# Squares of the norms added by VectorE, and post-norm factors read from PSUM, in a two-layer hybrid decoder trunk

## The chip, the cores and the metric

The kernel runs on one core of one Trainium2 chip (trn2). The metric is the device time of one execution in microseconds (us); lower is better. A core has five engines with a queue of their own each: TensorE (PE in the profile; its weight loads are PEld), VectorE (DVE), ScalarE (ACT), GpSimd (POOL) and SyncE (SP, which here issues DMAs). They work in parallel and wait for each other by semaphores; each engine takes its own instructions strictly in the order in which the program was written out.

## The reference

A trunk of two layers (DEPTH 2) over 528 tokens (16 learned meta tokens ahead of 512) with 1024 channels. Layer 0 mixes by forgetting attention (16 heads of 64), layer 1 by a gated DeltaNet (8 heads of 128); each layer ends in a gated FFN of width 2816 with a causal convolution. Every mixer and every FFN stands between two RMSNorms:

```python
def rmsnorm(x, g):
    xf = x.astype(jnp.float32)
    y = xf * lax.rsqrt(jnp.mean(xf * xf, axis=-1, keepdims=True) + EPS)
    return (y * g.astype(jnp.float32)).astype(x.dtype)
...
for i in range(DEPTH):
    a = rmsnorm(h, norm_mix_pre[i])
    m = forgetting_attention(a, ...) if i % 2 == 0 else gated_deltanet(a, ...)
    h = h + rmsnorm(m, norm_mix_post[i])
    f = conv_ffn(rmsnorm(h, norm_ffn_pre[i]), ffn_w_up[i], ffn_conv[i], ffn_w_down[i])
    h = h + rmsnorm(f, norm_ffn_post[i])
return h[:, N_META:]
```

## The kernel before

Activations lie transposed: 128 channels on the partitions, tokens along the free side, 8 such tiles (k = 0 to 7) for 1024 channels. The tokens are cut in two halves, of 272 and 256 columns (260 and 256 from the last mixer projection on). Each matrix product (`dense`, L312) is done in a high and a low part of both operands (`xh`, `xl` of the activations, `wh`, `wl` of the weights): three matmuls for each k, accumulated in one PSUM tile. Weights come by SP's DMAs (`w`, L284), are rounded by ACT (`wh`, L285) and their rest is made by DVE or POOL (`wl`, L292). A list of weight tiles is worked through for half 0 at once and for half 1 some tiles later (`push`, a lag of 4 or 6), so that PE has work for one half while the other half's results are finished.

Between two stages stands `boundary`, once for each half: after the attention's output projection (called boundary 1 below), after the first FFN (boundary 2), after the DeltaNet's output projection (boundary 3), and after the second FFN (the end, with no norm behind it). For a half it does the following.

- While the last projection's eight tiles `m` come out of PSUM (L465, L468 or L811 on DVE), ACT squares each (`sq`, L352; the first one goes straight into the sum, `ssq`, L349) and the squares are added into `ssq` (L353). After the eighth, `reduce` lets PE sum over the partitions (L342, into the PSUM tile `psn`).
- `inv` adds the epsilon on DVE (`nst`, L361), takes the power -0.5 on POOL (L363), lets PE spread the factors over the partitions (transposes into `psn`, L365), and ACT copies them from PSUM to SBUF (`r`, L367).
- For k = 0 to 7, DVE multiplies `m` by the post-norm's gain and `r` (`bt`, L411), adds this to the residual stream (`h`, L412), and, where a stage follows, `prenorm_tile` squares the new `h` (ACT, L352) into the next norm's sum (L353), makes `xh` (ACT, L377) and `xl` (DVE, L378). The next stage's matmuls take `xh` and `xl` as they come; the next norm's factor `r` is multiplied in only when their result leaves PSUM (`ub`, L748). That second `inv` runs after the eighth k.

`psn` tiles come from two PSUM rings of one bank each, used in turn. The program's order on each engine is set by a scheduler that plays the whole program through with its own estimates of durations; the DeltaNet stage, in addition, orders its work by a table of delays (`Flow`). So an edit in one place can move instructions elsewhere.

Of the kernel before, what the change touches and what calls it, by code (L numbers as in the profile page):

```python
# [13 lines left out]
ALU = mybir.AluOpType  # L14
# [90 lines left out]
def trunk(ctx, tc, h0, wflat, params, out):  # L105
    nc = tc.nc
# [103 lines left out]
    def ng(name, layer, k):  # L210
        c = pc[name] + layer * 8 + k
        return prm[:, c:c + 1]
# [106 lines left out]
    def tmp(name):  # L319
        return sm.tile([P, 272], F32, name=name, tag="tmp", bufs=4)  # L320

    def tmp2(name):
        return sm.tile([P, 272], F32, name=name, tag="tm2", bufs=5)

    def chunks(half):
        n = HALF[half][1]
        return (0, 128, n - 128) if n > 256 else (0, 128)
# [6 lines left out]
    class SumSq:  # L334
# [9 lines left out]
        def add(self, src, tmp=tmp):  # L344
            n, k = self.n, self.k
            self.k += 1
            if k == 0:
                self.acc = sm.tile([P, 272], F32, name="ssq", tag=f"ssq{self.half}")
                nc.scalar.activation(self.acc[:, :n], src, AF.Square)  # L349
                return  # L350
            sq = tmp("sq")
            nc.scalar.activation(sq[:, :n], src, AF.Square)  # L352
            nc.gpsimd.tensor_tensor(self.acc[:, :n], self.acc[:, :n], sq[:, :n], op=ALU.add)  # L353
            if k == KT - 1:
                self.reduce()

        def inv(self):
            half, n, ch, ps = self.half, self.n, chunks(self.half), self.ps
            w = len(ch)
            st = sm.tile([P, 8], F32, name="nst", tag=f"nst{half}", bufs=2)  # L360
            nc.vector.tensor_scalar(st[:, 0:w], ps[:, 0:w], EPS, None, op0=ALU.add)  # L361
            yst[half] = st
            nc.gpsimd.tensor_tensor(st[:, 4:4 + w], st[:, 0:w], mhalf[:, 0:w], op=ALU.pow)  # L363
            for j, c in enumerate(ch):
                nc.tensor.transpose(ps[:, 16 + c:16 + c + 128], st[:, 4 + j:5 + j].to_broadcast([P, P]), ident[:])  # L365
            r = sm.tile([P, 272], F32, name="r", tag=f"r{half}")
            nc.scalar.copy(r[:, :n], ps[:, 16:16 + n])  # L367
            return r

    def new_x(half, name):  # L370
        return take(half, name, F32R)


    def prenorm_tile(half, k, name, layer, xh, xl, ss):
        ss.add(h[half][:, k, :], tmp2)
        g = ng(name, layer, k)
        nc.scalar.activation(xh[:, k, :], h[half][:, k, :], AF.Identity, scale=g)  # L377
        nc.vector.scalar_tensor_tensor(xl[:, k, :], h[half][:, k, :], g, xh[:, k, :].bitcast(F32), op0=ALU.mult, op1=ALU.subtract)  # L378
# [21 lines left out]
        X[half] = (xh, xl, r)  # L400

    def boundary(half, m, ssm, post, pre):
        r = ssm.inv()
        n = HALF[half][1]
        last = pre is None
        if not last:
            xh, xl = new_x(half, "xh"), new_x(half, "xl")
            ss = SumSq(half)
        for k in range(KT):
            t = tmp2("bt")  # L410
            nc.vector.scalar_tensor_tensor(t[:, :n], m[:, k, :], ng(post[0], post[1], k), r[:, :n], op0=ALU.mult, op1=ALU.mult)  # L411
            nc.vector.tensor_tensor(h[half][:, k, :], h[half][:, k, :], t[:, :n], op=ALU.add)  # L412
            if not last:
                prenorm_tile(half, k, pre[0], pre[1], xh, xl, ss)
            else:
                s = max(HALF[half][0], NM)
                e = HALF[half][0] + n
                nc.sync.dma_start(out[:, k, s - NM:e - NM], h[half][:, k, s - HALF[half][0]:n])
        if not last:
            X[half] = (xh, xl, ss.inv())  # L420
# [29 lines left out]
    def out_proj(srcs, post, pre, reload, m, dropsrc):  # L450
        more = m[0] is not None
        ssm = [None, None]
        for mt in range(8):
            def fn(u, half, mt=mt):
                n = HALF[half][1]
                if m[half] is None:
                    drop(*X[half][:2])
                    m[half] = take(half, "m")
                oh, ol = srcs(half)
                ps = dense(u, half, lambda k: oh[:, k, :], lambda k: ol[:, k, :])  # L460
                if mt == 0:
                    ssm[half] = SumSq(half)
                mm = m[half][:, mt, :]
                if more:
                    nc.vector.tensor_tensor(mm, mm, ps, op=ALU.add)  # L465
                    ssm[half].add(mm)
                else:
                    nc.vector.tensor_copy(mm, ps)  # L468
                    ssm[half].add(ps)
                if mt == 4:  # L470
                    reload(half)
                if mt == 7:
                    dropsrc(half)
                    boundary(half, m[half], ssm[half], post, pre)
                    drop(m[half])
            push(nextu(), fn)
# [293 lines left out]
    def ffn(layer, post, pre):  # L770
        with ExitStack() as cx:
# [27 lines left out]
            def down(u, half, b, mt):  # L799
                n = HALF[half][1]  # L800
                j0 = sum(FB[:b])
                if b == 0 and mt == 0:
                    m[half] = take(half, "m")
                if b == 2 and mt == 0:
                    ssm[half] = SumSq(half)
                ps = dense(u, half, lambda k: acts[j0 + k, half][0], lambda k: acts[j0 + k, half][1])
                mm = m[half][:, mt, :]
                if b == 0:
                    nc.scalar.copy(mm, ps)
                else:  # L810
                    nc.vector.tensor_tensor(mm, mm, ps, op=ALU.add)  # L811
                if b == 2:
                    ssm[half].add(mm)
                    if mt == 7:
                        drop(*X[half][:2])
                        boundary(half, m[half], ssm[half], post, pre)
                        drop(m[half])
# [662 lines left out]
```

## Time and profile before

| | |
|---|---|
| time, median of 3 runs | 1604.43 us (1603.03 to 1607.17) |
| the profiled execution's own time | 1601.35 us |
| its span on the core | 1599.4 us |
| PE busy | 1525.8 us (95%) |
| DVE busy | 1123.4 us (70%) |
| ACT busy | 815.4 us (51%) |
| POOL busy | 495.8 us (31%) |
| mean granted PE clock | 0.977 |

Times in the profile are counted from the span's start. The profiled execution is 3.1 us faster than the median of the runs. A row of the timeline reads: start, duration, engine, line, operation, output and inputs, and in brackets how long the engine sat idle before it and what ended that. A row of the groups reads: line, engine, operation, names, shapes, count, then busy time and mean ns of one, then idle time before and its releaser. A row by windows gives, for a stretch, its length and the busy time of each engine with its instructions, the granted PE clock, and the DMA share.

### The profile page before, as it was taken

The numbers are of one execution on the slowest core, as the hardware profiler recorded it, in microseconds if no ns is written. First come the engines' busy times: TensorE is split into PE (matmuls) and PEld (weight loads), VectorE is DVE, ScalarE is ACT, GpSimd is POOL, SyncE is SP. The second block draws the span as 40 slices with busy tenths as digits, with TensorE's granted clock in tenths as the row PEclk, the third lists the DMA queues.
The fourth block names the chain that finished last, engine by engine and source line by source line (L and its number), as shares of the span: only waits on it lengthen the run. The fifth ranks groups of instructions, "written<-read, shape, count | busy, mean of one in ns | idle before, by whom it ended". The sixth has DMA issues, their size and how long they took to land.

```text
span 1599.4 us, 33295 instructions
## 1 busy us (share of the span) xinstructions
PE 1525.8 (95%) x12630; PEld 1486.8 (93%) x12630; DVE 1123.4 (70%) x2629; ACT 815.4 (51%) x1925; POOL 495.8 (31%) x993
## 2 busy tenths in 40 slices
PE   8999999999999999999789899899989999999996
PEld 6999999899999999999789798898989999999996
DVE  7888888948974675674978665676569864765764
ACT  6677777735643442343564456545456543432441
POOL 6434443025300010012556475654154200100112
PEclk9999999999999999999799998999999999999998
DMA  5232222422223222222323322222141323323321
GB/s 175 89 89 79 75 78 85 134 65 82 84 83 100 93 85 88 93 93 72 107 75 90 90 61 71 68 77 61 50 150 66 91 82 106 92 82 106 93 67 53
DMA packets 63327, 139.04 MB, mean 87 GB/s; under 512 B 18584, under 2 KB 31288, under 8 KB 62784
## 3 DMA queue, kind: packets, MB, share of 16 engines
q1 hardware_dynamic: 62544, 134.55, 28.1%
q8 instruction: 99, 1.62, 0.4%
q0 software_dynamic: 480, 2.15, 0.4%
q14 instruction: 60, 0.49, 0.1%
q10 hardware_dynamic: 144, 0.22, 0.0%
HBM read 131.54 MB, written 5.36 MB: 86 GB/s over the span
## 4 chain that ended last, share of the span: by engine, by line
PE 74%; DVE 11%; POOL 5%; DMA 4%; ACT 3%; issue 3%; SPq 1%; POOLq 0%; DVEq 0%; ACTq 0%
PE ps L312 65%; POOL PR L1177 2%; POOL RB L1178 2%; DVE h L412 1%; DVE bt L411 1%; DVE wl L292 1%; PE av L698 1%; DMA w<-wflat 1%; DVE cv L764 1%; DMA gcr<-gcd 1%; PE pt L678 1%; DVE xl L378 1%; ACT wh L285 1%; PE s L1277 1%; DVE qr L577 1%
## 5 line engine op out<-in xcount | busy, mean ns | idle before, releaser
L312 PE MATMUL ps<-xh,wh 128*128 128x256 f32 (+4 forms) x2464 | 717.6, 293 | 16.8 <-DVE ub L748 9.2
L312 PE MATMUL ps<-xl,wh 128*128 128x256 f32 (+4 forms) x2464 | 710.8, 289 | 3.4 <-DVE xl L378 3.0
L312 PE MATMUL ps<-xh,wl 128*128 128x256 f32 (+4 forms) x2464 | 713.6, 290 | 0.0
L312 PEld LDWEIGHTS ps<-xh,wh 128*128 128x128 f32 (+1 forms) x2464 | 469.6, 192 | 22.8 <-DVE ub L748 6.3
L312 PEld LDWEIGHTS ps<-xl,wh 128*128 128x128 f32 (+1 forms) x2464 | 471.1, 191 | 7.4 <-DVE xl L378 4.6
L312 PEld LDWEIGHTS ps<-xh,wl 128*128 128x128 f32 (+1 forms) x2464 | 471.1, 191 | 1.0
L285 ACT CAST wh<-w 128x1024 fp32r<-128x1024 f32 (+3 forms) x226 | 225.1, 997 | 189.5 <-PE ps L312 166.7
L292 DVE TENSOR_TENSOR wl<-w,wh 128x1024 fp32r<-128x1024 f32 (+4 forms) x191 | 220.6, 1156 | 99.3 <-ACT wh L285 98.7
L764 DVE SCALAR_TENSOR_TENSOR cv<-ub,prm,cv 128x256 f32<-128x256 f32 (+2 forms) x494 | 243.8, 498 | 38.4 <-ACT cv L755 29.5
L312 PE MATMUL ps<-ah,wl 128*128 128x256 f32 (+2 forms) x704 | 199.5, 284 | 0.0
L312 PE MATMUL ps<-ah,wh 128*128 128x256 f32 (+2 forms) x704 | 199.3, 283 | 0.0
L312 PE MATMUL ps<-al,wh 128*128 128x256 f32 (+2 forms) x704 | 199.1, 283 | 0.0
L755 ACT ACTIVATE cv<-ub,prm 128x256 f32<-128x256 f32 (+2 forms) x224 | 113.8, 511 | 146.3 <-DVE ub L748 146.2
L748 DVE TENSOR_TENSOR ub<-ps,r 128x256 f32<-128x256 f32 (+2 forms) x224 | 95.4, 428 | 101.5 <-PE ps L312 100.6
L353 POOL TENSOR_TENSOR ssq<-ssq,sq 128x256 f32<-128x256 f32 (+2 forms) x98 | 90.5, 926 | 144.5 <-ACT sq L352 143.0
L312 PEld LDWEIGHTS ps<-ah,wh 128*128 128x128 f32 x704 | 132.6, 189 | 0.0
L312 PEld LDWEIGHTS ps<-al,wh 128*128 128x128 f32 x704 | 132.5, 188 | 0.0
L312 PEld LDWEIGHTS ps<-ah,wl 128*128 128x128 f32 x704 | 132.4, 188 | 0.0
L751 POOL COPY cy<-ub 128x2 f32<-128x2 f32 (+1 forms) x112 | 38.0, 341 | 279.3 <-DVE ub L748 277.7
L292 POOL TENSOR_TENSOR wl<-w,wh 128x512 fp32r<-128x512 f32 x70 | 95.0, 1377 | 72.1 <-ACT wh L285 56.8
L747 POOL COPY ub<-cy 128x2 f32<-128x2 f32 (+1 forms) x112 | 31.3, 280 | 197.1 <-DVE cv L764 160.0
L786 ACT ACTIVATE gl<-cv 128x272 f32<-128x272 f32 (+2 forms) x88 | 36.7, 418 | 42.0 <-DVE cv L764 41.7
(308 smaller groups left out, 2454.5 us busy)
## 6 DMA issues: line engine op xcount, KB each, us to landing
w<-wflat SPq DMA_DIRECT2D x176, 512.0 KB, 3.5
w<-wflat SPq DMA_DIRECT2D x32, 448.0 KB, 3.3
cB<-cdram SPq DMA_DIRECT2D x16, 264.0 KB, 3.3
w<-wflat SPq DMA_DIRECT2D x16, 256.0 KB, 2.7
h<-h SPq DMA_DIRECT2D x8, 272.0 KB, 5.3
cB<-cdram SPq DMA_DIRECT2D x16, 136.0 KB, 3.0
h<-h SPq DMA_DIRECT2D x8, 256.0 KB, 5.0
AB<-dA SPq DMA_DIRECT2D x16, 128.0 KB, 3.2
```

Of the source, the lines that this page charges most:

```text
L285: nc.scalar.copy(wh[:], w32)
L292: eng.tensor_tensor(wl[:, c], w32[:, c], wh[:, c].bitcast(F32), op=ALU.subtract)
L312: tok(nc.tensor.matmul(o, w[:, a], r[:, c0:c1], start=(i == 0), stop=(i == tot - 1)))
L353: nc.gpsimd.tensor_tensor(self.acc[:, :n], self.acc[:, :n], sq[:, :n], op=ALU.add)
L747: nc.gpsimd.tensor_copy(ub[:, 0:c0], carry.pop(ft)[:, :c0])
L748: nc.vector.tensor_tensor(ub[:, c0:c0 + n], ps, r[:, :n], op=ALU.mult)
L751: nc.gpsimd.tensor_copy(c[:, :c0], ub[:, n:n + c0])
L755: nc.scalar.activation(cv, ub[:, c0:c0 + n], AF.Identity, scale=w[c0])
L764: nc.vector.scalar_tensor_tensor(cv, ub[:, i:i + n], w[i], cv, op0=ALU.mult, op1=ALU.add)
L786: nc.scalar.activation(g, cv, AF.Gelu_apprx_tanh)
L1177: nc.gpsimd.tensor_tensor(t, R3[:, 0:a, l:l + 1].to_broadcast([P, a, w]), A3[:, l:l + 1, l + 1:32].to_broadcast([P, a, w]), op=ALU.mult)
L1178: nc.gpsimd.tensor_tensor(R3[:, 0:a, l + 1:32], R3[:, 0:a, l + 1:32], t, op=ALU.subtract)
```

## The change

All 98 additions of squares into `ssq` go from POOL to DVE. The eight post-norm calls of `inv` (two halves at four boundaries) no longer let ACT copy the factors to SBUF: `bt` reads them from the PSUM tile `psn`. The six pre-norm calls keep the copy, and the power -0.5 stays on POOL. Lines behind the edits have numbers that are higher by 2 or 3: `xl` of the pre-norm is L380, `bt` L414, `h` L415, `ub` L751 in the changed kernel.

```diff
@@ SumSq.add
             nc.scalar.activation(sq[:, :n], src, AF.Square)
-            nc.gpsimd.tensor_tensor(self.acc[:, :n], self.acc[:, :n], sq[:, :n], op=ALU.add)
+            nc.vector.tensor_tensor(self.acc[:, :n], self.acc[:, :n], sq[:, :n], op=ALU.add)
@@ SumSq.inv
-        def inv(self):
+        def inv(self, copied=True):
...
+            if not copied:
+                return ps[:, 16:16 + n]
             r = sm.tile([P, 272], F32, name="r", tag=f"r{half}")
             nc.scalar.copy(r[:, :n], ps[:, 16:16 + n])
             return r
@@ boundary
-        r = ssm.inv()
+        r = ssm.inv(False)
```

The scheduler writes the engines' orders anew. Three places are shown.

DVE at boundary 2, in the middle of half 1's eight k (a 256-column round of `bt`, `h`, `xl`), before:

```order
L411 SCALAR_TENSOR_TENSOR bt<-m_7369,prm,r 128x256
L412 TENSOR_TENSOR h_5587<-h_5587,bt 128x256
L378 SCALAR_TENSOR_TENSOR xl_10686<-h_5587,prm,xh_10685 128x256
L411 SCALAR_TENSOR_TENSOR bt<-m_7369,prm,r 128x256
L748 TENSOR_TENSOR ub<-ps,r 128x272
```

The same place after:

```order
L414 SCALAR_TENSOR_TENSOR bt<-m_7365,prm,psn 128x256
L751 TENSOR_TENSOR ub<-ps,r 128x272
L353 TENSOR_TENSOR ssq<-ssq,sq 128x256
L415 TENSOR_TENSOR h_5585<-h_5585,bt 128x256
L380 SCALAR_TENSOR_TENSOR xl_10678<-h_5585,prm,xh_10677 128x256
```

An addition stands between each `bt` and the `h` that needs it, and the first `ub` of the next stage comes one round earlier: behind the seventh `bt` of half 1 and not behind the eighth.

DVE at the start of boundary 3 (from the power's input `nst` of half 0 to half 0's first `xl`; `m` are half 1's last projection tiles, `wl` are weights of the next FFN), before:

```order
L361 TENSOR_SCALAR nst<-psn 128x3
L292 TENSOR_TENSOR wl<-w_16674,wh 128x1024
L465 TENSOR_TENSOR m_15716<-m_15716,ps 128x256 x3
L292 TENSOR_TENSOR wl<-w_16716,wh 128x1024
L411 SCALAR_TENSOR_TENSOR bt<-m_15448,prm,r 128x260 x2
L292 TENSOR_TENSOR wl<-w_16761,wh 128x1024
L412 TENSOR_TENSOR h_16192<-h_16192,bt 128x260
L361 TENSOR_SCALAR nst<-psn 128x2
L412 TENSOR_TENSOR h_16192<-h_16192,bt 128x260
L411 SCALAR_TENSOR_TENSOR bt<-m_15448,prm,r 128x260
L378 SCALAR_TENSOR_TENSOR xl_16318<-h_16192,prm,xh_16317 128x260
```

After:

```order
L292 TENSOR_TENSOR wl<-w_16662,wh 128x1024
L361 TENSOR_SCALAR nst<-psn 128x3
L353 TENSOR_TENSOR ssq<-ssq,sq 128x256
L468 TENSOR_TENSOR m_15708<-m_15708,ps 128x256
L353 TENSOR_TENSOR ssq<-ssq,sq 128x256
...
L414 SCALAR_TENSOR_TENSOR bt<-m_15440,prm,psn 128x260 x2
L415 TENSOR_TENSOR h_16184<-h_16184,bt 128x260
L292 TENSOR_TENSOR wl<-w_16704,wh 128x1024
L353 TENSOR_TENSOR ssq<-ssq,sq 128x256
L415 TENSOR_TENSOR h_16184<-h_16184,bt 128x260
L292 TENSOR_TENSOR wl<-w_16749,wh 128x1024
L380 SCALAR_TENSOR_TENSOR xl_16308<-h_16184,prm,xh_16307 128x260
```

`nst` goes behind one `wl` more, and the first two `bt` go ahead of the `wl` that stood before them.

SP at the start of the DeltaNet stage (`gcd` and `gcr` carry the gates' running sums through DRAM, `w` are weights), before and then after:

```order
L284 DMA w_11346<-wflat 128x1024
L944 DMA gcd<-BG 8x528
L1040 DMA gcr<-gcd 128x272 x2
L284 DMA w_11513<-wflat 128x1024
L284 DMA w_11685<-wflat 128x1024
```

```order
L284 DMA w_11338<-wflat 128x1024
L947 DMA gcd<-BG 8x528
L284 DMA w_11505<-wflat 128x1024
L1043 DMA gcr<-gcd 128x272 x2
L284 DMA w_11677<-wflat 128x1024
```

One weight load goes ahead of the first two `gcr`. In the DeltaNet stage behind it, DVE, ACT and POOL have many neighbours swapped; in the FFNs the orders differ only by the moved additions and by small swaps around the boundaries.

## The prediction, made before the changed kernel was run

> **What bounds the kernel now.** I read the page first, then the busy time by windows, then the timeline at the boundaries.
>
> ```profile
> span 1599.4 us, 33295 instructions
> PE 1525.8 (95%) x12630; PEld 1486.8 (93%) x12630; DVE 1123.4 (70%) x2629; ACT 815.4 (51%) x1925; POOL 495.8 (31%) x993
> ```
>
> PE is 95% busy, so all that can be won or lost lies in the 73.6 us in which it is not, and in stretches with a lowered clock. The windows say where those are: the middle of the first FFN, boundary 2 from its first `bt` to the next stage's first `ub`, boundary 3 likewise, boundary 1, and the end after PE's last product.
>
> ```profile
> 395.00:755.00 360.00, 360.00 (x2945) 360.00 (x2943) 236.62 (x454) 148.82 (x275) 43.97 (x143) 1.00 0.28 88
> ...
> 759.40:789.30 29.90, 21.83 (x138) 18.65 (x136) 29.73 (x55) 17.12 (x39) 19.38 (x29) 0.81 0.34 108
> 1195.60:1222.80 27.20, 22.75 (x159) 21.92 (x159) 26.91 (x51) 14.96 (x34) 13.03 (x15) 0.84 0.23 78
> 367.20:388.00 20.80, 20.25 (x162) 19.62 (x161) 20.14 (x34) 11.57 (x25) 11.92 (x12) 1.00 0.37 124
> 1585.98:1599.40 13.42, 1.04 (x6) 0.71 (x6) 6.52 (x18) 0.79 (x2) 1.55 (x3) 0.66 0.26 87
> ```
>
> The columns are length, PE, PEld, DVE, ACT, POOL, clock. In the FFN PE is busy in all of 360 us, and DVE has 123 us to spare: the additions of the post-norm's squares that move to DVE there cost nothing, since PE's own matmuls cover them. At boundary 1 PE still works (20.25 of 20.80). At boundaries 2 and 3 it lacks 8.1 and 4.5 us and runs at a clock of 0.81 and 0.84, and DVE is busy in 99% of both: there DVE sets the pace. So the change has to be priced on DVE.
>
> But DVE's busy time there is not all work:
>
> ```profile
> 779.05 0.41 DVE L412 TENSOR_TENSOR h<-h,bt 128x256 f32<-128x256 f32 x1
> 779.39 0.49 DVE L378 SCALAR_TENSOR_TENSOR xl<-h,prm,xh 128x272 fp32r<-128x272 f32 x1
> 779.80 0.41 DVE L412 TENSOR_TENSOR h<-h,bt 128x256 f32<-128x256 f32 x1
> 780.14 0.47 DVE L411 SCALAR_TENSOR_TENSOR bt<-m,prm,r 128x256 f32<-128x256 f32 x1
> ...
> 783.90 0.47 DVE L411 SCALAR_TENSOR_TENSOR bt<-m,prm,r 128x256 f32<-128x256 f32 x1
> 784.41 0.84 DVE L412 TENSOR_TENSOR h<-h,bt 128x256 f32<-128x256 f32 x1
> ```
>
> ```profile
> 778.08 0.77 POOL L353 TENSOR_TENSOR ssq<-ssq,sq 128x272 f32<-128x272 f32 x1 [1.01 <-ACT sq L352]
> 780.80 0.80 POOL L353 TENSOR_TENSOR ssq<-ssq,sq 128x256 f32<-128x256 f32 x1 [1.95 <-ACT sq L352]
> ...
> 784.18 0.79 POOL L353 TENSOR_TENSOR ssq<-ssq,sq 128x256 f32<-128x256 f32 x1 [0.88 <-ACT sq L352]
> ```
>
> The same `h` takes 0.41 us while POOL stands still (778.85 to 780.80) and 0.84 us when POOL's addition is under way. It ends at 785.25, which is 0.28 after POOL's end (784.97): it waited for POOL and then ran. Only instructions with both tensors in SBUF are held; one that reads one tensor from PSUM runs through:
>
> ```profile
> 765.33 1.22 DVE L292 TENSOR_TENSOR wl<-w,wh 128x1024 fp32r<-128x1024 f32 x1
> 766.46 0.98 DVE L411 SCALAR_TENSOR_TENSOR bt<-m,prm,r 128x272 f32<-128x272 f32 x1
> 767.37 0.41 DVE L811 TENSOR_TENSOR m<-m,ps 128x256 f32<-128x256 f32 x1
> ```
>
> ```profile
> 765.30 2.77 POOL L353 TENSOR_TENSOR ssq<-ssq,sq 128x256 f32<-128x256 f32 x2 [1.29 <-ACT sq L352]
> ```
>
> POOL's pair of additions covers 765.30 to 768.07; in it `bt` takes 0.98 us and `m`, which reads PSUM, its usual 0.41. So an addition on POOL is paid for on DVE already, about as dearly as doing it there.
>
> **The change, part by part.** Unheld, consecutive rows overlap by 0.07 to 0.08 us (779.05 + 0.41 against 779.39), so from start to start `h` takes 0.34, `xl` and `bt` 0.40 (0.47 less 0.07), `wl` 1.14 (1.22 less 0.08), `m` 0.33 and `nst` 0.07. The new addition has `h`'s shape and operand types: 0.34 (bounds: 0.33, as `m`, and 0.41, the whole row without overlap).
>
> Boundary 2, from the first `bt` to the first `ub`:
>
> ```profile
> L412 DVE TENSOR_TENSOR h<-h,bt 128x272 f32<-128x272 f32 (+1 forms) x15 | 10.1, 681 | 0.2
> L411 DVE SCALAR_TENSOR_TENSOR bt<-m,prm,r 128x272 f32<-128x272 f32 (+1 forms) x16 | 10.1, 641 | 0.7 <-ACT r L367 0.7
> L378 DVE SCALAR_TENSOR_TENSOR xl<-h,prm,xh 128x272 fp32r<-128x272 f32 (+1 forms) x14 | 7.5, 533 | 0.0
> L292 DVE TENSOR_TENSOR wl<-w,wh 128x1024 fp32r<-128x1024 f32 x3 | 3.6, 1216 | 0.0
> ```
>
> Unheld, these rows with 4 `m` and 2 `nst` would be 15 x 0.34 + 16 x 0.40 + 14 x 0.40 + 3 x 1.14 + 4 x 0.33 + 0.14 = 22.0 us; they took 29.9, so about 7.9 us were waiting for POOL. In the new order the same stretch holds 15 additions, and one `bt`, `h` and `xl` less: 22.0 + 15 x 0.34 - 1.14 = 26.0. That is 3.9 us less. The copy that goes:
>
> ```profile
> 759.39 0.92 DVE L411 SCALAR_TENSOR_TENSOR bt<-m,prm,r 128x272 f32<-128x272 f32 x2 [0.68 <-ACT r L367]
> ...
> 789.28 0.43 DVE L748 TENSOR_TENSOR ub<-ps,r 128x272 f32<-128x272 f32 x1
> ...
> 789.76 0.60 PE L312 MATMUL ps<-xh,wh 128*128 128x272 f32 x1 [3.81 <-DVE ub L748]
> ...
> 759.57 1.05 ACT L285 CAST wh<-w 128x1024 fp32r<-128x1024 f32 x1 [0.21 <-PE ps L312]
> ```
>
> DVE sat idle for 0.68 here until the copy was done; the copy (0.37 at the end of the program, below) and its hop make 0.4 of it. Against this stands a new wait: an addition in DVE's queue needs ACT's square, and behind it wait the rest of the half's instructions and, with them, PE. Inside a round the square is in time, as ACT makes it while DVE does `xl` and `bt` (0.80); but where ACT has a `wh` cast of 1.05 ahead of the square DVE can stand still. ACT had three such casts here, of which the first is shown; bounds 0 to 3.1 us, and I take 1.3, one cast and a bit, since most of them stand beside a `wl` or an `m` that DVE has to do anyway. Boundary 2: -3.9 - 0.4 + 1.3 = -3.0 (bounds -4.3 to -1.2). It is passed on whole, as PE waits there 3.81 us for that `ub`.
>
> Boundary 3 starts late for another reason:
>
> ```profile
> 1190.75 1.23 DVE L292 TENSOR_TENSOR wl<-w,wh 128x1024 fp32r<-128x1024 f32 x1 [1.29 <-ACT wh L285]
> ...
> 1194.43 1.23 DVE L292 TENSOR_TENSOR wl<-w,wh 128x1024 fp32r<-128x1024 f32 x1 [1.46 <-ACT wh L285]
> 1195.57 1.35 DVE L411 SCALAR_TENSOR_TENSOR bt<-m,prm,r 128x260 f32<-128x260 f32 x2
> ...
> 1190.76 1.96 POOL L363 TENSOR_TENSOR nst<-nst,mhalf 128x3 f32<-128x3 f32 x1
> ...
> 1192.77 0.54 PE L365 MATMUL psn<-ident,nst 128*128 128x128 f32 x3 [1.33 <-POOL nst L363]
> ...
> 1223.27 0.39 PE L312 MATMUL ps<-xh,wh 128*128 128x256 f32 x1 [1.74 <-DVE ub L748]
> ```
>
> `nst` now goes behind the `wl` that ends at 1191.9, but POOL then has no additions queued ahead of the power; with 1.0 us for it (half of the 1.96, in which DVE's `wl` held it) and 0.5 for the transposes, `bt` can go at about 1194.0 instead of 1195.57, since the `wl` of 1194.43 and the copy no longer stand in front. Behind it the stretch to `ub` holds 12 additions, 14 `bt`, 14 `h`, 13 `xl`, 4 `wl` and 2 `nst`: 24.3 us against 27.2. On DVE that makes -1.5 - 2.9 = -4.4, but PE was short by only 4.5 us there, and its start follows half 0's first `xl`, which keeps its distance from `bt` (one `wl` more, fewer waits): -1.5. After that PE is at work until its late waits. So bounds are -4.4 and, with one cast's wait on top of the start, -0.5; I take -2.4, the start and half a `ub` wait of 1.74.
>
> Boundary 1: DVE's stretch shrinks likewise, but PE lacks only 0.55 in the 20.80 us: -0.3 (bounds -0.6 and +0.5).
>
> The end is the one place where nothing runs beside it:
>
> ```profile
> 1587.06 0.72 POOL L353 TENSOR_TENSOR ssq<-ssq,sq 128x256 f32<-128x256 f32 x1 [0.95 <-ACT sq L352]
> ...
> 1589.95 0.37 ACT L367 COPY r<-psn 128x256 f32<-128x256 f32 x1 [3.03 <-PE psn L365]
> ...
> 1590.35 2.07 DVE L411 SCALAR_TENSOR_TENSOR bt<-m,prm,r 128x256 f32<-128x256 f32 x5 [1.72 <-ACT r L367]
> ```
>
> The last addition takes 0.41 and not 0.72, and starts without POOL's 0.1 of queue: -0.4; the copy and its hop go (1589.95 to 1590.35): -0.4. Together -0.8 (bounds -1.0 and -0.5).
>
> What `bt` costs from PSUM no row shows. The nearest are two multiplications of one shape, of which one reads PSUM:
>
> ```profile
> L748 DVE TENSOR_TENSOR ub<-ps,r 128x256 f32<-128x256 f32 x112 | 47.2, 423 | 70.3 <-PE ps L312 70.1
> ...
> L794 DVE TENSOR_TENSOR cv<-cv,gl 128x256 f32<-128x256 f32 x44 | 18.6, 423 | 1.1
> ```
>
> 423 ns both: no surcharge; bounds of 5 ns either way over the 37 `bt` that count (15 + 14 + 8) make 0.2 us. [...]
>
> Holding `psn` until the eighth `bt` delays nobody: the bank's next writer is the next norm's sum, which needs the eighth `h` first. POOL loses 98 additions (the power comes through sooner); ACT loses 8 copies.
>
> Sum: -0.3 - 3.0 - 2.4 - 0.8 = -6.5 us. Against the profiled execution, 1601.35 - 6.5 = 1594.9; against the median, 1604.43, which lies 3.1 higher, **1598**.
>
> **The rivals.** First, *the DeltaNet stage gives it back*. It starts as much earlier as boundary 2 ends earlier, but a weight load now stands ahead of `gcr` on SP, and the DVE and ACT rows behind have changed places.
>
> ```profile
> 824.25 6.22 SPq L284 DMA_DIRECT2D w<-wflat  x2
> ```
>
> The second of two such loads held SP's queue until 830.5. If the load moved ahead does the same, `gcr`, on which DVE and all that follows it wait, comes up to 6 us late; with 5 of them on the chain, 1.5 of the 6.5 are left: about 1603. For it speaks that this stage is a chain; against it, that the first of the two went at once. Chance 0.28.
>
> Second, *DVE is slower for it*. If the long `h` were the price of following its `bt`, and not of POOL, nothing would be refunded: boundary 2 pays 15 x 0.34 = 5.1, less 1.5 for the round that goes behind `ub` (one `bt`, `h`, `xl` at the means above) and 0.4 for the copy, +3.2; boundary 3 pays 12 x 0.34 + 1.14 less 1.8 and the 1.5 of its start, +1.9; boundary 1, whose cover of 0.55 is used up by the same 3.6, +2; the end -0.8. Together +6.3: 1611. It decides from a `h` behind its `bt` that still takes over 0.65 with POOL idle. The rows at 779.80 and 784.41 speak against it. Chance 0.12.
>
> Third, *`bt` is dearer from PSUM*: if it could no longer overlap its neighbour by 0.07, 37 x 0.07 = 2.6 of the 6.5 go: 1600.5. Against it stand the two rows of 423 ns. Chance 0.05. [...]
>
> **How the numbers follow.** Forecast 0.55, the rivals 0.28, 0.12 and 0.05. A measurement of this kernel tells about 0.3% (4.8 us) from no change. The forecast's own range is 1595 to 1600.5 (the bounds halved), nearly all faster by that; 0.50 of its 0.55, and 0.04 from a mild first rival, make faster 0.54. Within 0.3%: the rest of the forecast and of the first and third rivals, 0.35. Slower: the second rival's upper half and a bad case of the first, 0.11. Range: down to 1592, where boundaries 2 and 3 give 4.3 and 4.4 and the DeltaNet stage a little more; up to 1606, the first rival with a full 6 us and a boundary that gives nothing.
>
> **What would show it.** `h` at 0.41 to 0.44 in nearly all of its 64 rows; DVE's stretch from `bt` to `ub` near 27 us at boundary 2 and 24 to 25 at boundary 3; no ACT wait of over 1 us ahead of L353 on DVE; the end after PE's last product 0.8 shorter; `bt` at 0.47 to 0.49. The prediction fails if `h` stays long, if L353 on DVE waits several us for ACT, or if the first `gcr` lands later after `gcd` than before.

## The result and the profile after

The changed kernel took 1591.41 us (median of 4 runs, 1587.79 to 1593.61) against 1603.73 us for the kernel before on the same chip (4 runs, 1602.45 to 1607.17): a ratio of 0.9915, 95% interval 0.9894 to 0.9937. The direction was forecast; the size was not: 12 us against 6.5, and the median lies 0.6 us under the range. Both kernels scatter by some 10 us from run to run (below), and nine more runs of the changed kernel gave 1595.83 us, ratio 0.9947, interval 0.9928 to 0.9965.

The head of the page, of the profiled execution (1592.99 us):

```profile
span 1591.2 us, 33230 instructions
PE 1525.4 (96%) x12630; PEld 1486.6 (93%) x12630; DVE 1131.1 (71%) x2727; ACT 809.8 (51%) x1917; POOL 402.2 (25%) x895
```

PE does the same work (1525.8 before); POOL lost 94 us, and DVE, with 98 instructions more, gained only 8: 98 x 0.34 = 33 us came and about 26 us of waiting went. The windows that answer to those of the prediction (length, PE, PEld, DVE, ACT, POOL, clock): boundary 2, boundary 3, boundary 1 and the end.

```profile
759.78:786.16 26.38, 22.24 (x141) 18.64 (x140) 26.25 (x67) 16.12 (x36) 3.52 (x9) 0.81 0.39 123
1189.66:1215.14 25.48, 22.19 (x159) 21.98 (x159) 24.36 (x60) 14.32 (x33) 2.51 (x2) 0.81 0.31 96
368.23:388.00 19.77, 19.77 (x165) 19.77 (x164) 18.90 (x43) 11.46 (x24) 0.70 (x1) 1.00 0.41 134
1578.10:1591.20 13.10, 1.50 (x9) 0.84 (x7) 6.91 (x19) 0.42 (x1) 0.69 (x1) 0.63 0.23 80
```

DVE is still busy in over 95% of boundaries 2 and 3, but no longer by waiting. Its groups of instructions at boundary 2, from the first `bt` to the first `ub` (busy us, mean ns):

```profile
L414 DVE SCALAR_TENSOR_TENSOR bt<-m,prm,psn 128x272 f32<-128x272 f32 (+1 forms) x15 | 7.0, 478 | 0.0
L353 DVE TENSOR_TENSOR ssq<-ssq,sq 128x256 f32<-128x256 f32 (+1 forms) x16 | 6.7, 420 | 0.0
L380 DVE SCALAR_TENSOR_TENSOR xl<-h,prm,xh 128x272 fp32r<-128x272 f32 (+1 forms) x13 | 6.3, 483 | 0.0
L415 DVE TENSOR_TENSOR h<-h,bt 128x272 f32<-128x272 f32 (+1 forms) x14 | 5.8, 422 | 0.0
```

`h` fell from a mean of 681 ns to 422, `bt` from 641 to 478, `xl` from 533 to 483, and DVE waits for ACT nowhere here. One round, start to start 0.41, 0.35, 0.35 and 0.41:

```profile
774.20 0.49 DVE L414 SCALAR_TENSOR_TENSOR bt<-m,prm,psn 128x272 f32<-128x272 f32 x1
774.61 0.43 DVE L353 TENSOR_TENSOR ssq<-ssq,sq 128x272 f32<-128x272 f32 x1
774.96 0.43 DVE L415 TENSOR_TENSOR h<-h,bt 128x272 f32<-128x272 f32 x1
775.31 0.49 DVE L380 SCALAR_TENSOR_TENSOR xl<-h,prm,xh 128x272 fp32r<-128x272 f32 x1
```

The stretch takes 26.4 us and not 29.9, and PE's wait for the first `ub` shrinks from 3.81 us to 1.72:

```profile
786.16 0.42 DVE L751 TENSOR_TENSOR ub<-ps,r 128x272 f32<-128x272 f32 x1
...
786.64 0.40 PE L312 MATMUL ps<-xh,wh 128*128 128x272 f32 x1 [1.72 <-DVE ub L751]
```

Where the time went by stage stands in the next table: three traces of each kernel (the first pair, and three more runs told of below). A boundary is counted here from PE's first sum of the squares (`psn` from `ssq`) to the first `ub` of the next stage.

| stage | before, us | after, us | mean change | forecast |
|---|---|---|---|---|
| start to boundary 1 | 361.6, 362.8, 362.8 | 363.1, 362.1, 362.7 | +0.3 | 0 |
| boundary 1 | 34.0, 33.6, 33.6 | 33.9, 33.9, 33.9 | +0.1 | -0.3, with the next |
| first FFN | 358.8, 358.8, 358.8 | 357.9, 357.9, 357.9 | -0.9 | |
| boundary 2 | 34.9, 34.9, 34.9 | 31.3, 31.9, 31.4 | -3.4 | -3.0 |
| DeltaNet | 397.4, 398.2, 397.6 | 397.3, 399.1, 399.7 | +0.9 | 0 |
| boundary 3 | 36.1, 35.6, 36.2 | 31.7, 31.7, 31.4 | -4.3 | -2.4 |
| second FFN | 365.0, 366.5, 366.5 | 364.8, 366.3, 364.8 | -0.7 | 0 |
| last sums to the end | 11.6, 12.1, 12.1 | 11.3, 11.3, 11.1 | -0.7 | -0.8 |
| all | 1599.4, 1602.5, 1602.5 | 1591.2, 1594.1, 1592.7 | -8.8 | -6.5 |

The boundaries repeat to within 0.6 us, so their terms can be read from one trace; the long stages move by up to 2.4 us of themselves.

Boundary 3 moved most. The rows of after, from the sums' `nst` to PE's wait for `ub`:

```profile
1187.53 0.15 DVE L361 TENSOR_SCALAR nst<-psn 128x3 f32<-128x3 f32 x1
...
1187.77 0.99 POOL L363 TENSOR_TENSOR nst<-nst,mhalf 128x3 f32<-128x3 f32 x1 [21.12 <-DVE nst L361]
...
1188.81 0.81 PE L365 MATMUL psn<-ident,nst 128*128 128x128 f32 x3 [2.28 <-POOL nst L363]
...
1189.66 0.88 DVE L414 SCALAR_TENSOR_TENSOR bt<-m,prm,psn 128x260 f32<-128x260 f32 x2 [0.32 <-PE psn L365]
...
1215.62 0.38 PE L312 MATMUL ps<-xh,wh 128*128 128x256 f32 x1 [0.93 <-DVE ub L751]
```

and of before, where POOL's queue held the power back behind two additions, from the `nst` of 1189.30 to 1190.76:

```profile
1189.30 0.15 DVE L361 TENSOR_SCALAR nst<-psn 128x3 f32<-128x3 f32 x1
...
1188.58 2.22 POOL L353 TENSOR_TENSOR ssq<-ssq,sq 128x256 f32<-128x256 f32 x2 [1.26 <-ACT sq L352]
```

From `nst` to the first `bt` it is 2.1 us now (1187.53 to 1189.66) and was 6.3 (1189.30 to 1195.57): the power starts 0.24 after `nst` and not 1.46, takes 0.99 and not 1.96, and `bt` follows the first transposes by 0.85 and not 2.8, for the copy and the `wl` in front of it are gone. Of these 4.1 us, 1.5 are given back because `nst` itself stands later after the sums. The `wl` ahead of `bt` weighs most: in e13, another trace of the kernel before, the power took only 0.88 us and `bt` still came 6.5 us after `nst`.

The end:

```profile
1579.34 0.42 DVE L353 TENSOR_TENSOR ssq<-ssq,sq 128x256 f32<-128x256 f32 x1 [0.54 <-ACT sq L352]
...
1579.91 0.58 PE L342 MATMUL psn<-oneD,ssq 128*128 128x1 f32 x4 [1.57 <-DVE ssq L353]
...
1582.23 2.05 DVE L414 SCALAR_TENSOR_TENSOR bt<-m,prm,psn 128x256 f32<-128x256 f32 x5 [1.55 <-PE psn L365]
```

### The profile page after: what moved, and what is told of

Read it like the earlier page. It is cut to its first block, busy times and chain, and to the rows that moved or that the text cites. A ratio compares the mean times of both kernels' runs of the same rounds, so it can differ in the third digit from the quotient of the medians.

```text
span 1591.2 us, 33230 instructions
## 1 busy us (share of the span) xinstructions
PE 1525.4 (96%) x12630; PEld 1486.6 (93%) x12630; DVE 1131.1 (71%) x2727; ACT 809.8 (51%) x1917; POOL 402.2 (25%) x895
## 4 chain that ended last, share of the span: by engine, by line
PE 77%; DVE 8%; POOL 5%; ACT 3%; issue 3%; DMA 3%; SPq 0%; POOLq 0%; DVEq 0%; ACTq 0%
PE ps L312 67%; POOL RB L1181 2%; POOL PR L1180 1%; DMA w<-wflat 1%; DVE cv L767 1%; PE av L701 1%; PE pt L681 1%; DVE bt L414 1%; DVE wl L292 1%; DMA gcr<-gcd 1%; ACT wh L285 1%; DVE h L415 1%; DVE qr L580 1%; PE o L1294 1%; PE sc L649 1%
## 5 line engine op out<-in xcount | busy, mean ns | idle before, releaser
L751 DVE TENSOR_TENSOR ub<-ps,r 128x256 f32<-128x256 f32 (+2 forms) x224 | 94.5, 427 | 92.6 <-PE ps L312 90.7
L363 POOL TENSOR_TENSOR nst<-nst,mhalf 128x3 f32<-128x3 f32 (+1 forms) x14 | 12.6, 900 | 201.0 <-DVE nst L361 200.8
```

Source lines behind the costliest of these rows:

```text
L751: nc.vector.tensor_tensor(ub[:, c0:c0 + n], ps, r[:, :n], op=ALU.mult)
```

## The experiments

Theory: GpSimd's additions hold VectorE's instructions that read two tensors from SBUF, and the change ends that. Rivals: the copy that went makes the gain; the long `h` was the price of following its `bt`; and, once the time was known, TensorE's clock makes the part beyond the forecast. Each series of runs had its own runs of the kernel before: medians 1602.82 (23 runs; the first four experiments), 1602.54 (14; the next four), 1604.24 (23; the next three) and 1601.69 us (16; the last four).

### The two halves of the change

```
e1:  r = ssm.inv()                    # copied again; squares on VectorE
e2:  nc.gpsimd.tensor_tensor(self.acc...)   # squares on GpSimd again; factors from PSUM
```

> All squares added by VectorE, the post-norm's factors still copied by ScalarE. Theory (VectorE's instructions with two SBUF tensors are held while GpSimd's addition runs; the gain is the end of that holding): nearly the whole gain stays, 1592 to 1595 us, 8 to 12 below the kernel before; only the wait for the copy, some 0.4 us at a boundary and 0.7 at the tail, comes back. Rival (the copy's wait and ScalarE's time make the gain): 1602 to 1604.

> The post-norm's factors read from PSUM, all squares still added by GpSimd. Theory of the holding: 1 to 2 us below the kernel before, 1602, with h at 0.84 us in the boundaries as before. Rival (the copy makes the gain): 1591 to 1594.

e1: 1592.31 us, ratio 0.9939 (0.9916 to 0.9962): the additions alone give about the whole gain. Boundary 2 took 31.0 us, boundary 3 34.0. e2: 1597.83 us, ratio 0.9972 (0.9956 to 0.9989): 4.5 us, between the two expectations, so reading the factors from PSUM does more than save a copy. Boundary 2 took 33.1 us, boundary 3 34.6. Its groups at boundary 2 show why:

```profile
L415 DVE TENSOR_TENSOR h<-h,bt 128x272 f32<-128x272 f32 (+1 forms) x15 | 9.1, 606 | 0.2
L380 DVE SCALAR_TENSOR_TENSOR xl<-h,prm,xh 128x272 fp32r<-128x272 f32 (+1 forms) x14 | 7.8, 554 | 0.0
L414 DVE SCALAR_TENSOR_TENSOR bt<-m,prm,psn 128x272 f32<-128x272 f32 (+1 forms) x16 | 7.5, 480 | 0.3 <-PE psn L365 0.3
```

POOL adds here as before, and `h` is still long (606), but `bt` is at 480 ns, down from 641: with its factor in PSUM it has one tensor in SBUF and is no longer held. That is 16 x 0.16 = 2.6 us of DVE at this boundary. Against the means of the table, at boundary 2 the halves are substitutes (3.9 and 1.8 us alone, 3.4 together); at boundary 3 each gives part (1.9 and 1.4 alone, 4.3 together). The early start there belongs to the factor in PSUM and the order that comes with it: `bt` comes 6.5 us after the sums in e2 and 8.2 in e1.

### Which squares

```
e3:  eng = nc.vector if tmp is tmp2 else nc.gpsimd    # pre-norm's on VectorE
e4:  eng = nc.gpsimd if tmp is tmp2 else nc.vector    # post-norm's on VectorE
```

> As the changed kernel, but only the squares of the pre-norm (inside the boundaries) are added by VectorE; those of the post-norm stay on GpSimd. Theory of the holding: the held instructions lie in the boundaries, so most of the gain stays, 1593 to 1596; h is long only where a post-norm's addition on GpSimd falls into a boundary. Rival (the additions' own latency on GpSimd ahead of a boundary, the chain from the last product to the factors, makes the gain): 1598 to 1602.

> The other half: only the post-norm's squares are added by VectorE, the pre-norm's by GpSimd. Theory of the holding: 1599 to 1602, with h held in the boundaries as before. Rival (latency ahead of the boundary): 1593 to 1596. The parts that this run and the one before it keep should add up to the whole gain if they do not need one another.

e3: 1592.73 us, ratio 0.9939 (0.9920 to 0.9957); e4: 1600.05 us, ratio 0.9976 (0.9957 to 0.9995), no more than e2 with no square moved. In the traces boundaries 2 and 3 took 31.8 and 31.5 us in e3, as in the changed kernel, and 33.2 and 33.8 in e4, near e2's 33.1 and 34.6. (The DeltaNet stage took 394.9 us in the one trace and 404.3 in the other; why is open.) The 42 additions of the pre-norms, all within boundaries, carry the gain; the 56 of the post-norms, though they are the most of what moved, give nothing that these runs can tell.

### GpSimd busy again, with nothing to wait for

Three kernels put work on GpSimd beside each of VectorE's pre-norm additions.

```
e6:  dj = tmp1("dj"); nc.gpsimd.tensor_tensor(dj[:, :n], sq[:, :n], sq[:, :n], op=ALU.add)
e7:  dj = tmp1("dj"); nc.gpsimd.memset(dj[:, :n], 0.0)
e9:  nc.gpsimd.tensor_tensor(cmask[:], sq[:, 0:P], prm[:, 0:P], op=ALU.add)
     nc.gpsimd.tensor_tensor(cmask[:], sq[:, P:2 * P], prm[:, 0:P], op=ALU.add)
```

> The changed kernel, and beside every pre-norm square that VectorE adds, GpSimd adds the same square to itself into a scratch tile that nobody reads (98 - 49 = some 49 additions of its old kind, without a reader). Theory of the holding: h, xl and the new additions, all with both tensors in SBUF, are long again (means of 0.55 to 0.75 in the boundaries), bt stays at 0.48 since its factor comes from PSUM, boundary 2 grows from 26.4 to 30 to 33 us, and the time is 1599 to 1605. Rival (the long h was the price of following its bt): 1591 to 1594, h at 0.42.

> As the run before, but GpSimd only fills the scratch tile with zeros: it writes and reads nothing. If it is GpSimd's reads that hold VectorE, h stays at 0.42 to 0.45 and the boundaries at 26 to 27 us; if any access of GpSimd's does, h is at 0.5 to 0.8.

> The changed kernel, and beside each pre-norm square that VectorE adds GpSimd makes two additions of 128x128, each of a half of that square, into a table that nobody reads any more. The orders of VectorE, ScalarE and the weight loads are the same to the row as in the changed kernel, so only GpSimd's use of SBUF differs. Theory of the holding: wherever GpSimd's addition runs, h, xl and ssq take 0.6 to 0.9 and end some 0.3 after it, bt (PSUM) stays at 0.47 to 0.49; about 35 pairs of 0.6 to 0.7 us in the boundaries, of which some half fall on a holdable instruction that the end waits for: 1599 to 1606. Rival (h is long for following its bt, GpSimd doesn't matter): 1592 to 1597, as the changed kernel.

e6 took 1627.24 us (ratio 1.0149, 1.0127 to 1.0170), more than the theory allowed, and settles nothing: its program came out in another order (half 0's boundary ahead of all of half 1's, with TensorE idle for 10.6 us at boundary 1), its 42 additions lie elsewhere, and `h` was mostly short. e9 was made for that: its orders on VectorE and ScalarE are the changed kernel's to the row. It took 1606.58 us (ratio 1.0014, 0.9995 to 1.0034): with GpSimd busy again the whole gain is gone, though the new order, with `ub` a round earlier, is kept. Boundaries 1, 2 and 3 took 35.3, 34.9 and 35.6 us, 1.4, 3.4 and 3.9 above the changed kernel's means: together 8.7, as much as the table's whole gain. The DeltaNet stage took 404.5 us in this trace, 5.8 above the changed kernel's mean; that was not taken apart, and the run traced was 4 us slower than the median. The rows of DVE and POOL in e9:

```profile
786.31 0.68 DVE L418 TENSOR_TENSOR h<-h,bt 128x256 f32<-128x256 f32 x1
786.91 0.68 DVE L383 SCALAR_TENSOR_TENSOR xl<-h,prm,xh 128x256 fp32r<-128x256 f32 x1
787.51 0.47 DVE L417 SCALAR_TENSOR_TENSOR bt<-m,prm,psn 128x256 f32<-128x256 f32 x1
...
785.97 0.74 POOL L355 TENSOR_TENSOR cmask<-sq,prm 128x128 bf16<-128x128 f32 x1
786.79 0.52 POOL L356 TENSOR_TENSOR cmask<-sq,prm 128x128 bf16<-128x128 f32 x1
787.59 0.46 POOL L355 TENSOR_TENSOR cmask<-sq,prm 128x128 bf16<-128x128 f32 x1 [0.28 <-ACT sq L352]
```

`h` ends at 786.99 and `xl` at 787.59, each 0.28 after the POOL row that ran beside it (786.71, 787.31), as in the trace of before. Of the 43 `h` and `xl` in the trace that began while one of these additions had 0.1 us or more to run, 41 end 0.28 to 0.30 after it. `bt` takes its 0.47, though its row here began 0.08 ahead of POOL's. In e2, where GpSimd's additions are longer, 18 of the 64 `bt` began while one was running; none took more than 0.50 us, and 14 of them ended before it, as this one:

```profile
1198.76 0.47 DVE L414 SCALAR_TENSOR_TENSOR bt<-m,prm,psn 128x260 f32<-128x260 f32 x1
...
1198.62 0.74 POOL L353 TENSOR_TENSOR ssq<-ssq,sq 128x260 f32<-128x260 f32 x1 [1.68 <-ACT sq L352]
```

Nobody reads what POOL makes in e9, so no dependency is left that could explain the wait; the rival of the dependency on `bt` falls. e7, whose GpSimd writes and doesn't read, took 1592.14 us in its one run, with `h` at 0.42 and boundary 2 at 31.8. Its orders on VectorE and ScalarE are the changed kernel's, too, but its fills run bunched, and only six of VectorE's `h`, `xl` and additions began beside one. None of them was longer than usual; this addition ran amid six fills and ended before the last of them:

```profile
770.23 0.43 DVE L355 TENSOR_TENSOR ssq<-ssq,sq 128x272 f32<-128x272 f32 x1
...
769.23 1.56 POOL L358 MEMSET dj<- 128x256 f32 x6
```

So in the few rows that tell, a writer holds nobody.

e10 is e9 with ScalarE's copy back, so that `bt` reads its factor from SBUF.

```
e10: r = ssm.inv()      # beside e9's two additions
```

> The same two additions on GpSimd, beside the kernel that adds on VectorE but keeps ScalarE's copy, so that bt has both tensors in SBUF (orders as in that kernel). If the place of the factor decides whether bt can be held: bt's mean over the boundaries 0.55 to 0.65, against 0.48 in the run before this, and the time 2 to 5 us above it. If bt is not held in either, 0.48 to 0.50 in both.

It took 1608.23 us in its one run, 1.7 above e9's median, which one run cannot tell from nothing. Its orders are e1's, and against e1 its boundaries are 4.0, 4.9 and 3.3 us longer (37.9, 35.9 and 37.3). `bt`'s mean at boundary 2 was 528 ns against 478 in e9, less than expected, since only some of them meet a POOL row; one that does:

```profile
783.90 0.69 DVE L417 SCALAR_TENSOR_TENSOR bt<-m,prm,r 128x272 f32<-128x272 f32 x1
...
783.76 0.53 POOL L356 TENSOR_TENSOR cmask<-sq,prm 128x128 bf16<-128x128 f32 x1
```

It ends 0.30 after POOL's end (784.59 and 784.29). So the place of the factor does decide whether `bt` can be held.

### The sums without anybody's additions

```
e8:  for j, c in enumerate(ch):      # pre-norm: TensorE sums each square itself
         nc.tensor.matmul(self.ps[:, j:j + 1], sq[:, c:c + 128], oneD[:], start=..., stop=...)
```

> The pre-norm's squares are added by nobody: TensorE sums each of them straight into the norm's PSUM columns (8 x 3 or 8 x 2 small products instead of 3 or 2), the post-norm's squares stay on VectorE, and its factors are copied by ScalarE, as the bank must come free. VectorE loses 15 x 0.34 = 5.1 us at boundary 2 and 4.1 at boundary 3 against the changed kernel; TensorE gains 35 products of 0.12 us a boundary, 4 us, where it lacked 5 to 8. If VectorE sets the pace of the boundaries: 1583 to 1589. If TensorE's wait for each square in its own queue takes it back: 1590 to 1598.

1619.70 us, ratio 1.0112 (1.0082 to 1.0142): neither case. The price was set too low:

```profile
L352 PE MATMUL psn<-oneD,sq x240: 163/251/372, 375.2 to 1230.4; 128*128 128x1 f32 x120
```

```profile
375.23 0.72 PE L352 MATMUL psn<-oneD,sq 128*128 128x1 f32 x6
```

Each float32 sum is two products on TensorE, so there are 240 of 0.12 us (0.72 for six), 28.8 us at full clock, of which 3.6 replace the sums that went; the time is 23.9 us above that of the changed kernel in the same series. That the two are so close is partly chance. Boundary 1 with the first FFN took 6.6 us more, with the clock at 1.00 while the sums ran; boundary 2 and the DeltaNet stage took about as long as in the changed kernel (31.1 and 400.4 us); boundary 3 with the second FFN took 15 to 17 more, for there the clock was at half for 30.7 us in all (1199 to 1209 and 1213 to 1233), against 6.8 to 10.2 us in the traces of the changed kernel, though TensorE was busy in all of the second stretch:

```profile
1220.00:1230.00 10.00, 10.00 (x49) 10.00 (x48) 7.25 (x18) 6.66 (x14) 1.30 (x3) 0.50 0.00 1
```

What VectorE was spared shortened boundary 1 (31.5 us for 33.9) and hardly the others (31.1 for 31.5 and 33.2 for 31.6).

### Chance and TensorE's clock

> The changed kernel once more, for a steadier median and a second trace. If the 12 us between the medians are the change's, the ratio stays at 0.990 to 0.993 and the profiled execution shows the same length of the boundaries; if a part was chance, it moves to 0.994 to 0.996 (the sum of the terms, 6.5 to 8 us). The mean granted clock is to be read beside it: 0.979 in the four runs so far, against 0.975 in 23 of before.

e5 is the changed kernel again: 1595.83 us (9 runs, 1590.71 to 1599.10), ratio 0.9947 (0.9928 to 0.9965). So a part of the first 12 us was probably chance: four runs of either kernel are few when the runs of one kernel lie 10 us apart.

What they scatter with is the granted clock: over the 76 runs of the kernel before that came with the experiments, the time falls by 1.1 us for each 0.001 of mean clock (correlation -0.86). In the first series the fastest run of the kernel before (1597.32 us) had a mean clock of 0.978, the slowest (1608.33 us) of 0.972. In the traces the clock is either 1.00 or 0.50, and lower for about 3.4 us or a multiple of it (3.4, 6.8 or 10.2 us in the first trace of either kernel, but for the stretch at the program's end). Two traces of the kernel before show the same place, TensorE's wait of 1.74 us for `ub` after boundary 3. In the first, where TensorE went on at 1223.27, the clock held, and 36 products lie in the 4 us from 1225:

```profile
1225.00:1229.00 4.00, 4.00 (x36) 4.00 (x35) 3.10 (x9) 3.74 (x8) 0.94 (x3) 1.00 0.00 0
```

In e13, the same program, it did not, and 24 lie there:

```profile
1224.38 0.39 PE L312 MATMUL ps<-xh,wh 128*128 128x256 f32 x1 [1.74 <-DVE ub L748]
...
1225.00:1229.00 4.00, 4.00 (x24) 4.00 (x23) 3.11 (x8) 2.83 (x6) 1.66 (x5) 0.57 0.01 4
```

The second FFN, where TensorE never waits, took 366.5 us in e13 and 365.0 in the first trace: one such period costs 1.5 us. (In the table, the three traces with the period have 366.3 to 366.5, the three without it 364.8 to 365.0.) So the same wait of 1.74 us had a half-rate period of 3.4 us behind it in one execution and none in the other; what decides that, no run shows.

The next runs asked whether the change gains by the clock, too: the wait at the start of the DeltaNet stage (3.81 us before, 1.72 after) had half-rate periods behind it before the change and none after.

> The kernel before, for a second trace. If the gain beyond the boundaries is the clock: TensorE waits about 3.8 us for ub at the start of the DeltaNet stage, half-rate periods of 3.4 us or more follow at once, and the DeltaNet stage from the first ub to the norm's sums takes 399 to 405 us, though the first trace had 397.4. If it is not, 396 to 398.

> The kernel before, for a third trace; the same as for the second.

> The changed kernel, for a third trace: the wait at the start of the DeltaNet stage is at most 1.8 us, no half-rate period begins within 5 us of it, and the DeltaNet stage takes 396 to 400 us; boundaries 2 and 3 from the norm's sums to ub are 31.3 to 32.0 and 31.5 to 32.0.

The times were 1604.23, 1604.46 and 1594.37 us. The half-rate period is there in both traces of the kernel before (792 to 795, after waits of 4.00 and 4.04 us) and missing in the changed one, as expected. But the DeltaNet stage took 398.2 and 397.6 us before and 399.7 after, against 399 to 405 and 396 to 400: it isn't shorter. At its start TensorE waits for VectorE again soon (3.66 us for `ub` at 817 in e13), so a half clock there costs nothing. Nor do the boundaries gain by it: their half-rate stretches are the same in both kernels, 10.2 us at boundary 2 in all six traces, and 10.2, 6.8 and 6.8 at boundary 3. This rival falls as a cause of the gain in the boundaries; as a cause of the scatter the clock stands. Over whole executions the changed kernel's mean clock was a little higher (0.977 in e5's nine runs, 0.975 in the 14 beside them), and whether that is chance is open.

Two kernels tried to hold the clock at boundary 3 by products that fill TensorE's wait for the power.

```
e11: for i in range(16): nc.tensor.matmul(ps[:, 400:401], allD[:], oneD[:], ...)   # one column
e12: for i in range(6):  nc.tensor.matmul(ps[:, 300:428], allD[:], ident[:], ...)  # 128 columns
```

> The changed kernel with 16 small products (0.12 us each, into a PSUM column that nobody reads) ahead of the transposes of each half's factors at boundary 3, where TensorE waits 2.3 us for the power and then 2.9 for the last sums. If the half clock there follows from this idle time, the half-rate stretch of 7 to 10 us from 1188 to 1200 gets shorter by 3.4 or more; if TensorE's rate sets boundary 3's end, the time falls by 1.5 to 3.5 us (1592 to 1594 against 1595.8), if VectorE sets it, it stays at 1594 to 1597.

> As the run with the 16 one-column products, but 6 products of 128 columns (into PSUM columns that nobody reads, some 0.25 us each, 1.5 us in all) ahead of the transposes of each half's factors at boundary 3. If the clock goes by how much the array computes and not by whether TensorE has an instruction, these hold it where the narrow ones did not: the half-rate stretch at 1188 to 1206 shrinks to 7 us or less, and the time is 1592 to 1596; if no product helps, it is 10 us or more and the time is 1595 to 1600.

e11: 1600.75 us, ratio 0.9982 (0.9960 to 1.0004), slower than either case. Its fillers were 32 products a half, 6.2 and 7.0 us, not 1.9, and put the transposes off; and the clock stayed at half from 1188 to 1205, though TensorE was busy nearly all the time:

```profile
1190.00:1198.00 8.00, 7.26 (x35) 7.18 (x36) 5.87 (x12) 4.49 (x8) 0.81 (x1) 0.50 0.48 143
```

e12: 1593.50 us, ratio 0.9955 (0.9937 to 0.9973), no different from the changed kernel. Its half-rate stretch (1191 to 1198, 6.8 us) is shorter than e11's 17.1, but three traces of the changed kernel without fillers have 10.2, 6.8 and 6.8. Boundary 3 took 33.2 us in its trace against 31.4 to 31.7 without fillers, and `bt` came 7.6 us after the sums, not 6.0 to 6.3; in the time of its runs the wide products neither cost nor bring anything that can be told. Whether narrow products fail to hold the clock is open: in e8 it was at half beside them at boundary 3, as here, but at 1.00 beside them at boundary 1.

No version beat the changed kernel beyond its interval: e1, e3 and e12 lie within it.

## Why the prediction was off

*What held.* The mechanism: `h` at 0.42, `bt` at 0.48, the additions at 0.42 with 0.34 from start to start, no surcharge for PSUM (`bt` 128x256 476 ns in e5 against 483 in e1, where its factor is in SBUF), and VectorE as the bound of the boundaries. Boundary 2 was forecast at -3.0 and gave -3.4; the end -0.8 and -0.7; the DeltaNet stage 0 and +0.9, within its scatter. The first rival (the stage gives it back) needed +5 there, and the first `gcr` went out 1.5 us after `gcd` in either kernel; the second (dependency) and the third (dear `bt`) needed rows that aren't there.

*The step that failed is the term of boundary 3*: -2.4 taken, -4.3 measured. That this is nearly the bound of -4.4 is luck, as the bound was made of other parts (-1.5 and -2.9, where -2.6 and -1.8 were measured). The term was mis-sized in two places. The start was put at 1194.0, 7.3 us after the sums (1186.69), since `nst` was to wait for a `wl` that ends at 1191.9, 5.2 us after the sums. In the traces of after `nst` did run behind that `wl`, but the `wl` itself ended 4.2, 4.5 and 4.2 us after the sums, about a microsecond earlier than its time taken from the profile before, and `bt` came 6.2, 6.3 and 6.0 us after the sums, against 8.9, 8.3 and 9.0 before. That is -2.6 for -1.5. And of VectorE's shorter stretch only half a wait for `ub` (0.9) was passed on, because TensorE lacked just 4.5 us in the window that began with `bt`. But TensorE stood still ahead of that window, too (1.33 us before its transposes of 1192.77), and the next stage's `ub` stands at the end of VectorE's stretch in either kernel: the stretch, 27.2 us before and 25.5 after, was passed on whole, -1.8. The cap on the stretch cost about a microsecond, the time of the `wl` another.

*Smaller.* Boundary 1 with the first FFN gave -0.8 for -0.3, the same 0.9 in the FFN in all three pairs of traces; no run took it apart. At boundary 2 the copy's 0.4 didn't show (`bt` came 5.0 us after the sums in both kernels), and the 1.3 us of waiting for ACT's casts didn't either (idle 0.0 ahead of all additions there). That `bt` would no longer be held when its factor is in PSUM was in the prediction's own rule and not in its sum: it changes nothing where the additions leave GpSimd as well, but in e2 it is 2.6 us of VectorE's time at boundary 2 alone. In the second rival's sum the round is put at 1.5 us, where the means that it names give 1.9, and the +2 of boundary 1 stands without a working; nothing that decided against this rival hangs on either.

*The range.* The traces make the change -8.8 us, and from the 76 runs of the kernel before that came with the experiments (medians of 1601.7 to 1604.2, 1603.0 over all) that is 1594.2: inside 1592 to 1606, as is the second median of 1595.83. The first median, 1591.41, lies 2.8 us below that. Its four runs had a mean clock of 0.979 against 0.977 in e5, which at 1.1 us for each 0.001 makes about half of the 4.4 us between the two medians; the rest stays open. The forecast started from 1604.43, the median of three runs. The bounds of its terms, all at their best, give 1594; the range went 2 us below that for a quicker DeltaNet stage and held nothing for the runs' own scatter of some 10 us.

## What to carry to other kernels

Price an addition on GpSimd by what it holds up on VectorE: where VectorE set the pace with instructions on two SBUF tensors, moving the addition to VectorE cost 0.34 us each and paid back more (boundary 2 went from 34.9 to 31.5 us), and the factor read from PSUM took `bt` out of the contention (480 ns in e2, 641 before) without making it longer (476 ns in e5, 483 in e1). Only the squares inside the boundaries mattered; the 56 others could have stayed. When a wait is passed along, look at whether the waiting engine still waits at the end of the stretch, not at how much it stands still in between; and give a range room for the scatter of the runs that it will be held against.

## What the runs showed of the hardware that was not expected

- GpSimd's additions, which read SBUF, held VectorE's instructions on two SBUF tensors: in e9, 41 of the 43 `h` and `xl` that began beside one with 0.1 us or more to run ended 0.28 to 0.30 us after it. Its fills of 128x256, which only write (e7, six in 1.56 us), held none of the six that began beside one.
- TensorE's clock fell to half for 3.4 us after an idle time of 1.74 us in e13, and not after the same idle time in the first trace of that kernel; in the second FFN, where TensorE never waits, one such period cost 1.5 us.
- A busy TensorE is no warrant of a full clock: amid one-column products it was shown busy for 7.26 of 8 us in e11 and for 10.00 of 10.00 in e8 at a clock of 0.50; elsewhere in e8 the clock was at 1.00 beside the same products.
- A float32 sum into one PSUM column was two products, 0.24 us at a full clock, which made 120 of them (28.8 us of TensorE) dearer than the 42 additions of 0.34 us that they replaced.
